# Layer 0's feed-forward of a hybrid S5, retention and attention block: side work at 0.36 and 0.7 steps per yield in place of 0.5 and 0.9

## The chip, the cores and the metric

The kernel runs on one core of a Trainium2 chip, as one program. The metric is the time of the program on the device in microseconds. The kernel before took 1546.05 us, the median of 3 runs (1538.01 to 1549.89).

## The reference, cut to what matters

Two layers work on 256 latent and 256 context tokens of width 1024, all in float32. What bears on the change: each layer's modulation (shift, scale and gate, for both halves of the layer) is a product of two vectors with a 1024 x 6144 matrix; each layer's S5 mixer needs tables that depend on parameters alone; and each layer ends with a SwiGLU feed-forward of hidden width 2816.

```python
for l in range(DEPTH):                       # DEPTH = 2
    mod = (silu_c @ w_ada[l] + b_ada[l])[:, None, :]
    mod_c = silu_cc @ w_ada[l] + b_ada[l]
    sh1, sc1, g1, sh2, sc2, g2 = jnp.split(mod, 6, axis=-1)
    h = rms_norm(x) * (1.0 + sc1) + sh1      # the same for ctx with mod_c
    u, rk, rv, nk, nv, rq, rg, nq, gates = split_cols(h @ w_in[l], IN_SPLIT)
    y_s5, y_s5_c = s5_mixer(u, cu, s5_lam_re[l], ..., need_ctx)
    ...                                      # retention and neighbourhood attention
    x = x + g1 * merge_branches(y_s5, y_ret, y_na, gates, ...)
    x = x + g2 * swiglu(rms_norm(x) * (1.0 + sc2) + sh2, w_ffn_gate[l], w_ffn_up[l], w_ffn_down[l])
return rms_norm(x) * final_norm

def s5_discretize(lam_re, lam_im, log_dt, b_re, b_im): ...   # powers of A and A-scaled B: the tables
def swiglu(h, w_gate, w_up, w_down):
    return (jax.nn.silu(h @ w_gate) * (h @ w_up)) @ w_down
```

In layer 0 the feed-forward is done for both streams (512 tokens), in layer 1 for the latent tokens alone.

## The kernel before, in words

**Products.** Every large product is made of three passes. A weight tile of 128 x 1024 values is loaded by SP's queue (line 377) into one of four raw buffers that are used in turn; ScalarE rounds it into a high part (387), VectorE takes the low part as the difference (388), into one of three pairs of buffers; and TensorE multiplies high by high, high by low and low by high (393 to 395). A product of one weight tile with 512 tokens is 24 matmuls.

**The feed-forward** (`ffn`, 1752) is a generator. For three groups of 8, 8 and 6 hidden tiles it makes the gate and the up projection of each tile, activates and multiplies them (1775 to 1780), and then adds the down projection of the group to the stream (`to_stream`, 1715; residual, 1711). The last down projection of layer 0 leaves its last three output tiles for the end and does them for the context half first, then calls the norm of layer 1 on that half, then does the latent half. It yields after each projection, once for both of the first tile. Behind the feed-forward, layer 1 begins with the norm of the latent half (962), the rest of the last table generator (965), and the first two projections of its keys (971), whose first half of columns needs the context norm alone.

**Side work.** Two chains of steps are woven into layer 0's feed-forward at line 1024. `weave` (204) adds a rate to a counter for each yield of the main generator, and takes one step of the side for each whole unit; what is left when the main generator has ended is done at once:

```python
    for _ in main:
        for i, (_, each) in enumerate(sides):
            acc[i] += each
            while live[i] and acc[i] >= 1.0:
                acc[i] -= 1.0
                step(i)
    while any(live):
        ...
```

The first side, `rest` (1019), makes layer 1's S5 tables. `s5_e` (764) is a state table of a block of groups: one step of six VectorE instructions (756, 757, 759, for two directions), then four steps of four transposes and a copy (776, 778). `s5_kwins` (1181) takes two steps for each of four blocks: a window table of six VectorE instructions (756, 757, 761) from two loaded inputs (683 to 685), then 32 small matmuls (1165), copies, and stores of the window (1178) and of the table (1192). `rest` has the transposes of block 0, blocks 1 and 2 whole, the four windows, and the first step of block 3: 4 + 5 + 5 + 8 + 1 = 23 steps. The transposes of block 3 are what layer 1 does at line 965.

The second side is layer 0's last gate (`ada`, 554; 5 steps) and then `ada_sum` (558) for five of layer 1's six pieces of the modulation. A piece is eight chunks of the matrix. Each chunk is loaded into one of the same four raw buffers, and scaled and added into two accumulators, one for each stream: by ScalarE for the first chunk (568), by VectorE for the others (570, two instructions of 128 x 1024). A ninth step closes the piece with 16 small matmuls (576), a copy, two transposes (540) and the bias (546).

**The order of the instructions.** The order in which the generators run is the order of the program. The framework's planner (`schedule_with_timeline_sim`, 1811) sets each engine's own order from it. Buffers in `fa` are handed out in turn from one arena, so a new buffer waits until what stood in its place has been read.

Of the kernel before, what the change touches and what calls it, by code (L numbers as in the profile page):

```python
# [203 lines left out]
def weave(main, *sides):  # L204

    acc = [0.0] * len(sides)
    live = [True] * len(sides)

    def step(i):
        try:  # L210
            next(sides[i][0])
        except StopIteration:
            live[i] = False
# [8 lines that stand above are left out]
        for i in range(len(sides)):  # L222
            if live[i]:
                step(i)
# [6 lines left out]
def chain(*gens):  # L231
    for g in gens:
        yield from g


class Net:
# [676 lines left out]
    def layer(self, l):  # L913
# [6 lines left out]
        if l == 0:  # L920
# [15 lines left out]
            ada = self.ada(0, (2, 3, 4, 5))  # L936
# [24 lines left out]
        else:  # L961
# [13 lines left out]
            ada = self.adas  # L975
# [18 lines left out]
        ada = self.adas  # L994
        if last:
            ada = self.ada(1, (5,))
            for _ in self.m_out(l):
                pass
            F.cursor = 8192
            self.norm(l, 1, [2, 3])  # L1000
            self.fill(ada, 2, 1)
            weave(self.ffn(l), (ada, 0.5))
        else:
            e = []

            def ahead():
                self.tabs[1] = F.alloc(1280, "p2", top=True), F.alloc(1040, "BB", top=True)
                for blk in range(4):
                    self.et[blk] = F.alloc(2048, "et", top=True)
                b2 = self.s5_tables(1)  # L1010
                yield
                e.extend(self.s5_e(1, b2, blk) for blk in range(4))
                next(e[0])
                yield

            weave(self.m_out(l, lambda: self.norm(l, 1, [0, 1])), (ahead(), 0.5))
            self.norm(l, 1, [2, 3])

            def rest():
                yield from chain(e[0], e[1], e[2], self.s5_kwins(1))  # L1020
                next(e[3])

            self.adas = self.ada_sum(1, range(5))
            weave(self.ffn(l, lambda: self.norm(l + 1, 0, [0, 1])), (rest(), 0.5), (chain(ada, self.adas), 0.9))
            self.e_left = e[3]
        self.dump(f"xffn{l}", self.xT)

# [816 lines left out]
```

## Time and profile before

| | |
|---|---|
| runs shown | 1538.01, 1546.05, 1549.89 us |
| the profiled execution | 1546.39 us, span 1544.6 us |
| TensorE busy | 1492.7 us, 97% of the span |
| VectorE busy | 984.1 us, 64% |
| ScalarE busy | 626.9 us, 41% |
| DMA queue of the weights (q1) | 247.36 MB, 48.4% of 16 engines' span |

The times in the rows are microseconds from the start of the span, on one core. Engines are PE (TensorE matmuls), PEld (its weight loads), DVE (VectorE), ACT (ScalarE), POOL (GpSimd) and SP (the queue that issues loads and stores); a q behind a name is the engine's own queue of waits. Layer 0's feed-forward lies between about 600 and 987 us.

### The profile page before, as it was taken

The page shows a single profiled execution, that of the slowest core. Times are in us where ns is not written, and L with a number is a line of the kernel's source. Part 1 is how long each engine was busy: PE and PEld are TensorE (multiplying, and loading weights), DVE is VectorE, ACT ScalarE, POOL GpSimd, SP SyncE. Part 2 cuts the span into 40 slices and gives each one's busy share as a digit, 9 for nine tenths or more (in the row PEclk, how much of TensorE's full clock was granted, in tenths as well). Part 3 has the DMA queues.
Part 4 walks back from the last instruction along what each step waited for, and adds up shares of the span by engine and source line. Part 5 has one row for each costly group of instructions (what it writes and reads, how often), then busy time and mean ns, then how long its engine had stood idle before and what let it go on. Part 6 is the DMA issues. An engine that isn't in the chain of part 4 may idle for free. (4 is left out here: it accounts for less than half of the span.)

```text
span 1544.6 us, 25494 instructions
## 1 busy us (share of the span) xinstructions
PE 1492.7 (97%) x10066; PEld 1269.3 (82%) x10066; DVE 984.1 (64%) x1729; ACT 626.9 (41%) x1121; POOL 259.5 (17%) x612
## 2 busy tenths in 40 slices
PE   7998898999999999999999999999999999999997
PEld 5886676788888888787887788898689899899997
DVE  6884754445356686598599974732565676665666
ACT  4554443334312334332322322454654355444443
POOL 6206996000000000000000000007991000000000
PEclk9999899999999999999999999999999999999999
DMA  9514456873332533455466642432325667555552
GB/s 369 190 55 141 159 208 176 278 258 113 123 102 69 164 96 111 167 186 178 153 205 214 230 160 65 157 123 75 101 83 161 230 225 271 179 192 184 171 190 98
DMA packets 80760, 255.35 MB, mean 165 GB/s; under 512 B 9216, under 2 KB 23040, under 8 KB 77824
## 3 DMA queue, kind: packets, MB, share of 16 engines
q1 hardware_dynamic: 78016, 247.36, 48.4%
q10 hardware_dynamic: 2304, 4.20, 0.8%
q0 software_dynamic: 320, 2.16, 0.6%
q8 instruction: 79, 1.29, 0.3%
q14 instruction: 41, 0.34, 0.1%
HBM read 230.68 MB, written 20.84 MB: 163 GB/s over the span
## 5 line engine op out<-in xcount | busy, mean ns | idle before, releaser
L393 PE MATMUL psall<-ra 128*128 128x256 f32 (+1 forms) x2122 | 711.3, 340 | 6.1 <-ACT ra L387 2.4
L394 PE MATMUL psall<-ra 128*128 128x256 f32 (+1 forms) x2122 | 709.0, 336 | 0.0
L395 PE MATMUL psall<-ra 128*128 128x256 f32 (+1 forms) x2122 | 707.4, 336 | 1.0 <-DVE ra L388 1.0
L388 DVE TENSOR_TENSOR ra<-fa,ra 128x1024 fp32r<-128x1024 f32 (+1 forms) x284 | 344.8, 1216 | 293.1 <-ACT ra L387 285.9
L387 ACT CAST ra<-fa 128x1024 fp32r<-128x1024 f32 (+1 forms) x284 | 293.7, 1038 | 557.9 <-PE psall L394 336.0
L393 PEld LDWEIGHTS psall<-ra 128*128 128x128 f32 x2122 | 401.7, 191 | 63.2 <-issue 10.7
L395 PEld LDWEIGHTS psall<-ra 128*128 128x128 f32 x2122 | 404.0, 191 | 44.9 <-issue 2.7
L394 PEld LDWEIGHTS psall<-ra 128*128 128x128 f32 x2122 | 405.2, 191 | 39.0 <-issue 1.3
L1109 POOL TENSOR_TENSOR fa<-fa 128x64 f32<-128x64 f32 x252 | 106.1, 442 | 137.4 <-ACT fa L1083 127.7
L1064 POOL MEMSET fa<- 128x32 f32 x2 | 0.2, 123 | 730.2 <-DVE ra L846 730.2
L570 DVE SCALAR_TENSOR_TENSOR fa<-fa 128x1024 f32<-128x1024 f32 x70 | 87.6, 1281 | 9.3 <-DMA fa<-in_wst_dram 7.6
L887 PE MATMUL psall<-ra 128*128 128x512 f32 x192 | 77.8, 414 | 0.2 <-ACT fa L1051 0.2
L888 PE MATMUL psall<-ra 128*128 128x512 f32 x192 | 76.2, 397 | 0.0
L1711 DVE SCALAR_TENSOR_TENSOR fa<-psall,fa 128x256 f32<-128x256 f32 x96 | 43.2, 480 | 51.3 <-PE psall L395 51.1
L889 PE MATMUL psall<-ra 128*128 128x512 f32 x192 | 75.3, 399 | 0.3 <-DVE ra L846 0.3
L1112 POOL TENSOR_TENSOR fa<-fa 128x64 f32<-128x64 f32 x126 | 58.2, 462 | 0.0
L1113 POOL TENSOR_TENSOR fa<-fa 128x64 f32<-128x64 f32 x126 | 53.8, 427 | 9.9
L887 PEld LDWEIGHTS psall<-ra 128*128 128x128 f32 x192 | 43.7, 229 | 8.0 <-issue 2.0
L889 PEld LDWEIGHTS psall<-ra 128*128 128x128 f32 x192 | 43.4, 229 | 6.5 <-DVE ra L846 0.8
L756 DVE TENSOR_TENSOR fa<-fa 128x1024 f32<-128x1024 f32 (+1 forms) x32 | 41.1, 1316 | 11.2 <-PE psall L1165 8.8
L888 PEld LDWEIGHTS psall<-ra 128*128 128x128 f32 x192 | 44.2, 230 | 4.9
L757 DVE TENSOR_TENSOR fa<-fa 128x1024 f32<-128x1024 f32 (+1 forms) x32 | 41.0, 1292 | 2.7 <-DMA fa<-in_s5c_dram 2.7
(242 smaller groups left out, 1380.5 us busy)
## 6 DMA issues: line engine op xcount, KB each, us to landing
fa<-in_wst_dram SPq DMA_DIRECT2D x364, 512.0 KB
gsp<-fa SPq DMA_DIRECT2D x8, 1152.0 KB
fa<-gsp SPq DMA_DIRECT2D x8, 1152.0 KB
fa<-in_wst_dram SPq DMA_DIRECT2D x16, 384.0 KB
xsp<-fa SPq DMA_DIRECT2D x2, 2048.0 KB
tgs<-fa ACTq DMA_DIRECT2D x16, 256.0 KB
fa<-kws SPq DMA_DIRECT2D x32, 128.0 KB
fa<-tgs SPq DMA_DIRECT2D x16, 256.0 KB
```

The costliest lines, as they stand in the source:

```text
L387: nc.scalar.copy(hi[:, :n], t[:, :n])
L388: nc.vector.tensor_tensor(out=lo[:, :n], in0=t[:, :n], in1=hi[:, :n].bitcast(F32), op=ALU.subtract)
L393: mm(out, wh, xh, start=start, stop=False)
L394: mm(out, wh, xl, start=False, stop=False)
L395: mm(out, wl, xh, start=False, stop=stop)
L570: nc.vector.scalar_tensor_tensor(out=acc[s].ap, in0=t, scalar=c, in1=acc[s].ap, op0=ALU.mult, op1=ALU.add)
L887: mm(o, xh, hi[:, ws], start=(kk == 0), stop=False)
L888: mm(o, xh, lo[:, ws], start=False, stop=False)
L889: mm(o, xl, hi[:, ws], start=False, stop=(kk == 7))
L1109: e.tensor_tensor(out=t[:, i], in0=at(pf, pr), in1=tab[:, i * 64:(i + 1) * 64].rearrange("p (r d g) -> p r d g", r=2, d=2), op=ALU.mult)
L1112: e.tensor_tensor(out=at(cf, cr), in0=at(cf, cr), in1=t[:, 0], op=ALU.add)
L1113: e.tensor_tensor(out=at(cf, cr), in0=at(cf, cr), in1=mk(T[s % 2], 96, [[-32, 2], [16, 2], [1, 16]]), op=ALU.add)
```

## The change

Both rates at which the side work is woven into layer 0's feed-forward are lowered: that of the tables from 0.5 to 0.36 steps per yield, and that of the last gate and the weighted sums from 0.9 to 0.7. Nothing else is changed.

```diff
             self.adas = self.ada_sum(1, range(5))
-            weave(self.ffn(l, lambda: self.norm(l + 1, 0, [0, 1])), (rest(), 0.5), (chain(ada, self.adas), 0.9))
+            weave(self.ffn(l, lambda: self.norm(l + 1, 0, [0, 1])), (rest(), 0.36), (chain(ada, self.adas), 0.7))
             self.e_left = e[3]
```

## Rows read from the trace of the kernel before

**Rows 1.** Page: the span, and busy time of each engine over it.

```profile
span 1544.6 us, 25494 instructions
...
PE 1492.7 (97%) x10066; PEld 1269.3 (82%) x10066; DVE 984.1 (64%) x1729; ACT 626.9 (41%) x1121; POOL 259.5 (17%) x612
```

**Rows 2.** Stretches of layer 0's feed-forward and the border behind it, all engines.

```profile
core 0: us, PE busy (x) PEld busy (x) DVE busy (x) ACT busy (x) POOL busy (x), PEclk, DMA share, GB/s
640.00:760.00 120.00, 120.00 (x564) 97.12 (x563) 87.71 (x96) 39.31 (x51) 0.00 (x0) 1.00 0.52 169
760.00:885.00 125.00, 122.39 (x660) 96.72 (x659) 116.03 (x127) 36.59 (x48) 0.00 (x0) 1.00 0.64 214
885.00:952.00 67.00, 67.00 (x309) 54.67 (x308) 39.89 (x48) 18.70 (x25) 0.00 (x0) 1.00 0.40 133
952.00:987.00 35.00, 35.00 (x209) 31.22 (x208) 18.95 (x40) 12.90 (x24) 0.00 (x0) 1.00 0.28 87
987.00:1007.00 20.00, 17.19 (x117) 16.32 (x116) 18.31 (x56) 11.78 (x25) 0.25 (x2) 0.91 0.53 198
```

**Rows 3.** Source lines: duration min/median/max, first and last start, L1711 from 848 on.

```profile
L1711 DVE SCALAR_TENSOR_TENSOR fa<-psall,fa x16: 471/476/484, 854.4 to 887.0; 128x256 f32<-128x256 f32 x16
...
L570 DVE SCALAR_TENSOR_TENSOR fa<-fa x70: 1276/1280/1286, 640.6 to 907.7; 128x1024 f32<-128x1024 f32 x70
...
L756 DVE TENSOR_TENSOR fa<-fa x14: 1214/1351/1358, 617.4 to 881.0; 128x1152 f32<-128x1152 f32 x8, 128x1024 f32<-128x1024 f32 x6
```

**Rows 4.** Stretches, the middle product line L394 alone: TensorE and its weight loads.

```profile
840.00:880.00 40.00, 18.15 (x47) 8.76 (x47) 1.00 0.66 223
880.00:952.00 72.00, 40.46 (x104) 19.33 (x103) 1.00 0.40 135
```

**Rows 5.** Stretches, the weighted sum L570 alone: VectorE, clock, DMA.

```profile
760.00:885.00 125.00, 39.51 (x32) 1.00 0.64 214
885.00:952.00 67.00, 12.48 (x10) 1.00 0.40 133
```

**Rows 6.** Groups of VectorE instructions by shape, 590 to 990 us.

```profile
L570 DVE SCALAR_TENSOR_TENSOR fa<-fa 128x1024 f32<-128x1024 f32 x70 | 87.6, 1281 | 9.3 <-DMA fa<-in_wst_dram 7.6 <-ACT fa L568 1.4
L388 DVE TENSOR_TENSOR ra<-fa,ra 128x1024 fp32r<-128x1024 f32 x61 | 74.5, 1222 | 37.0 <-ACT ra L387 37.0
...
L761 DVE SCALAR_TENSOR_TENSOR fa<-fa 128x1152 f32<-128x1152 f32 x8 | 11.3, 1412 | 0.0
L757 DVE TENSOR_TENSOR fa<-fa 128x1152 f32<-128x1152 f32 x8 | 10.8, 1352 | 0.0
L756 DVE TENSOR_TENSOR fa<-fa 128x1152 f32<-128x1152 f32 x8 | 10.7, 1353 | 1.4 <-PE psall L1165 1.4
...
L757 DVE TENSOR_TENSOR fa<-fa 128x1024 f32<-128x1024 f32 x6 | 7.3, 1219 | 0.0
L759 DVE TENSOR_TENSOR fa<-fa 128x1024 f32<-128x1024 f32 x6 | 7.3, 1219 | 0.0
L756 DVE TENSOR_TENSOR fa<-fa 128x1024 f32<-128x1024 f32 x6 | 7.1, 1218 | 0.4 <-PE psall L776 0.4
```

**Rows 7.** Timeline of TensorE, 846 to 860 us.

```profile
849.81 1.11 PE L1165 MATMUL psall<-fa 128*32 128x128 f32 x30 [0.32 <-DVE fa L761]
...
851.93 1.07 PE L576 MATMUL psall<-fa 128*32 128x256 f32 x16 [1.01 <-DVE fa L1171]
...
858.02 0.50 PE L395 MATMUL psall<-ra 128*128 128x512 f32 x1 [1.03 <-DVE ra L388]
```

**Rows 8.** Waits of SP's queue, 600 to 1010 us: total, times, longest.

```profile
SPq L377 <- DVE fa L570: 69.0, 33, 3.8
...
SPq L1178 <- DVE fa L1174: 8.5, 4, 3.4
```

**Rows 9.** Timeline of ScalarE, 840 to 862 us.

```profile
846.07 0.60 ACT L1775 ACTIVATE fa<-psall 128x512 f32<-128x512 f32 x1 [10.51 <-DVE fa L757]
```

**Rows 10.** Stretch of the border ahead of the feed-forward, columns as in rows 2.

```profile
580.00:600.00 20.00, 17.73 (x141) 14.89 (x139) 15.03 (x48) 9.93 (x19) 0.00 (x0) 0.87 0.43 136
```

## The prediction

> **What bounds the kernel now.** I read the page first, then the feed-forward of layer 0 by stretches of time, then the instructions that the change moves, and last the waits. The span is 1544.6 us and TensorE is busy for 97% of it [rows 1]; the profiled execution took 1546.39 us, 0.3 above the median of the runs shown, so the sum below, made against 1546.4, holds for the median as well. TensorE is the bound, so a new order of the side work can only give back time in which TensorE stood still, or take more.
>
> The reader should look in the stretches for where that is [rows 2]. TensorE is busy without a break from 640 to 760 and from 885 to 987 us. It loses time in two places: between 760 and 885 (122.39 of 125), and at the border to layer 1, 987 to 1007 (17.19 of 20, clock 0.91). VectorE tells why. From 760 to 885 it is busy for 116.03 of 125 us, 93%: there the tables of the four convolution windows and the modulation sums fall together. Behind that, from 885 to 987, it does 39.89 + 18.95 = 58.8 of 102 us, so 43.2 us are free. From 987 to 1007, under the norm that opens layer 1, it is busy for 18.31 of 20: nothing more fits there. So the quiet stretch stands just ahead of a full one, and the change fills the quiet one.
>
> **What is moved, and by how much.** The feed-forward of layer 0 yields 66 times: 15, 16 and 12 for its three groups of hidden columns, and 8, 8 and 7 for the down projections behind them. The table side needs 23 steps. At 0.5 it ends at yield 46, at 0.36 at yield 64 (23 / 0.36 = 63.9). The sums are 50 steps: 5 for layer 0's last gate and 9 for each of five pieces. At 0.9 they end at yield 56. At 0.7 they would need 71.4 yields, so only 46 steps are out at yield 66; the last three chunks of the fifth piece and its closing product come after the feed-forward, **ahead of the norm of line 962**. The sums do not end with it; they run over. Nothing is added or removed: the same instructions, loads and stores are issued in another order.
>
> Yield 47 is the end of the second down projection, whose residuals run to 887.0 [rows 3]. So yields 47 to 66 are the stretch from 885 to 987. A projection is eight triples of matmuls at 0.692 us (104 in 72 us, from 880 to 952 [rows 4]), 5.5 us, one yield. VectorE's work there changes so:
> - Out of it go the 10 weighted sums that stand in it now, 12.5 us [rows 5], and the rest of the fourth state table, 2 x 1.219 [rows 6]: 15 us.
> - Into it come steps 34 to 50 of the sums. The first chunk of a piece is a product on ScalarE, so these are 14 chunks of two instructions: 28 x 1.281 = 35.9 us [rows 6].
> - Three of the four window tables, each 2 x (1.353 + 1.352 + 1.412) = 8.23 us, 24.7 in all, and the whole fourth state table, 2 x (1.218 + 1.219 + 1.219) = 7.3 us [rows 6].
> - In all 67.9 - 15 = 52.9 us more, against 43.2 us free: 9.7 too many, if everything stays in its place.
>
> It does not all stay there. In the trace work starts ahead of its place when VectorE is free: the last weighted sum, due at yield 55 (885 + 8 x 5.5 = 929 us), starts at 907.7, and the first table instruction, due at yield 10 (11 for the first yield of two projections and 9 x 5.5, from 600: about 660), at 617.4 [rows 3]. At 21 us, which is 2.7 steps of the new rate, the sums take 2.36 two-instruction chunks out, 6.1 us; and the first of the three tables, due at yield 48, fits into 760 to 885, which has room: of its 116.0 us go 39.5 of sums [rows 5], 32.9 of window tables and 4.9 of the fourth state table, and 31.4 of sums (14 steps) and 8.2 of one table come, 78.3 in all. That is 9.7 - 6.1 - 8.2 = 4.6 us to spare. But VectorE was busy for 93%, not 100%, where it was fullest. At 93% 102 us hold 94.7, and 7.3 - 4.6 = **2.7 us** spill past 987, where every microsecond of VectorE delays the norm that TensorE waits for. Bounds: 0, and 9.7 + 7.3 = 17.0 if nothing moves ahead. I take 2.7, since these rows show work moving ahead.
>
> **What is given back.** Between 760 and 885 the free time of TensorE is 2.6 us. By spacing it is more: from 840 to 880 there are 47 triples [rows 4], 47 x 0.692 = 32.5 us, and with two blocks of 30 small matmuls at 1.11 and 16 at 1.07 [rows 7] 35.8 us are accounted for, 4.2 lost. The waits there name VectorE: the split of a weight (L388) 1.03 and the end of a window (L1171) 1.01 [rows 7]. I take 2.6 of 4.2 (bounds 0 and 4.2), because the fuller late stretch can bring part of the same waits back.
>
> **The rest.** The weight splits of layer 1's first two projections, 2 x 1.222 [rows 6], come behind the norm in the order of the program: 0 while they find gaps in its chain, 2.4 if not; I take 0, as the chain's gaps hold them now. TensorE's own side products move and stay as many; they cost the same. Also moved later are the four stores of windows and four of tables, and the loads of table inputs, on SP. A window's store holds weight loads queued behind it, 8.5 us in four, longest 3.4, and the sums hold them 69.0 us in 33 [rows 8]; three weight buffers, two projections of work ahead, cover that now, and 3.4 is the price where the cover is gone. POOL has no part (nothing in these stretches before 987 [rows 2]). The two accumulators of the sums stay allocated to the end, so other buffers come round sooner; such a reuse made ScalarE wait 10.51 us for a table instruction once [rows 9]. This is priced with the spill.
>
> The border already runs at 0.91 of the clock for 20 us after 2.8 us of idle time, 1.8 us lost (3.6 us at 1.2 GHz in place of 2.4); the border ahead of the feed-forward shows 0.87 after 2.3, 2.6 lost [rows 10]. Between 760 and 885 the clock stays at 1.00 in spite of the 2.6 idle. I add 0 for the clock: more idle time did not go with a lower clock in these two. Bounds 0 and 2.6. The Trainium skill, "TensorE: Matmul & The Clock Gate", section "HAM oscillation — how this bites in real kernels", speaks against the change: idle stretches between bursts of matmuls bring the clock down to half, and it is paid again on the way up. By that rule, idle time gathered at the border costs once more what it costs there now, an estimate of 1.8 us, and the sum would be 1548.3 and not 1546.5.
>
> **Sum:** 1546.4 - 2.6 + 2.7 = 1546.5; I say **1547**.
>
> **Rivals.**
> 1. *Spill at the border* (slower). VectorE keeps the sums' tail and the fourth state table in front of the norm; nothing moves ahead because buffers are not free. 17.0 + 2.4 + 2.6 - 2.6 = 19.4, so 1565.8 at the worst; with half of the spill, 8.5 + 2.4 + 1.8 - 2.6, 1556.5. It decides once VectorE has more than about 95 us of work between 885 and 987. For it: 18.31 of 20 behind, and the tail that runs over. Against: work starts 21 to 43 us early now.
> 2. *All waits go* (faster). Nothing spills, 4.2 come back in the middle and 1 of the 2.8 at the border: 1541.2. For it: from 640 to 987 VectorE has 262.6 of 347 us of work with either order, 76% [rows 2]. Against: the border's waits are a chain, not a load. "Perfetto Trace Analysis", section "Optimization Strategy", of the Trainium skill says that interleaving stretches with different limits may help; the trace shows only these 4.2 us to be had by it.
> 3. *It does not do what it says*: since the order of instructions follows when they can start, the new rates change little of what runs when: 1546, plus or minus 2.
>
> **Numbers.** Forecast (cancelling) 0.50, rival 1 0.27, rival 2 0.13, rival 3 0.10. About 1% (15.5 us) is what a measurement can tell from no change. More than that faster would need more idle time than 760 to 1007 holds (2.6 or 4.2, and 2.8, and 1.8 of clock): 0.03. Slower by over 1% is the upper part of rival 1, and stalls that a new order brings later in layer 1: 0.16. Within: 0.81. The range goes from rival 2 less half the spread of the runs shown, 1537, to 1563, most of rival 1.
>
> **What would show it.** Right: VectorE near 75 to 90 of 125 us from 760 to 885 and above 90 of 102 from 885 to 987; window tables and weighted sums still after 930; no idle TensorE in the middle; 3 to 6 us idle at the border. Wrong: weighted sums among the norm's instructions with more than 10 us of idle TensorE behind them, or tables still early with the same waits in the middle.

## The result, and the profile after

The kernel after takes 1555.18 us, the median of 20 runs (1546.37 to 1557.95); the kernel before, in 20 runs beside it, 1541.95 (1533.94 to 1549.89). The ratio is 1.0073, with a 95% interval from 1.0058 to 1.0087: 0.7% slower, about 11 us (the two medians alone lie 13.2 us apart). That lies inside 1% and inside the range, but it is not nothing. The profiled execution of after took 1550.7 us, 4.5 below its median, and that of before 4.4 above its own, so the two traces differ by only 4.3 us. In the trace of after layer 0's feed-forward starts 4.9 us earlier (608.4 against 613.3), in a part that the change does not touch; from there on after is 9.1 us longer.

The page of after: the span and each engine's busy time, as [rows 1].

```profile
span 1548.8 us, 25486 instructions
...
PE 1492.8 (96%) x10066; PEld 1271.6 (82%) x10066; DVE 988.9 (64%) x1729; ACT 627.3 (41%) x1121; POOL 259.6 (17%) x612
```

TensorE did the same work in the same busy time; the new microseconds are idle. The stretches of after show where, with the columns of [rows 2]:

```profile
760.00:885.00 125.00, 125.00 (x603) 100.63 (x602) 90.99 (x102) 36.16 (x46) 0.00 (x0) 1.00 0.51 174
885.00:952.00 67.00, 67.00 (x361) 53.84 (x360) 50.98 (x60) 21.98 (x31) 0.00 (x0) 1.00 0.51 162
952.00:987.00 35.00, 28.03 (x206) 23.75 (x206) 34.44 (x47) 10.38 (x20) 0.00 (x0) 0.87 0.75 267
987.00:1007.00 20.00, 14.87 (x83) 13.53 (x84) 15.84 (x56) 9.59 (x22) 0.25 (x2) 0.72 0.08 30
```

Between 760 and 885 us TensorE no longer stands still (125.00 of 125, against 122.39), and VectorE came down from 116.03 to 90.99. From 952 to 1007 TensorE is idle for 12.1 of 55 us, at 0.87 and 0.72 of the clock; before it was 2.8, at 1.00 and 0.91. By source line, with the columns of [rows 3], first the residual from 848 us on and then the weighted sum:

```profile
L1711 DVE SCALAR_TENSOR_TENSOR fa<-psall,fa x24: 462/472/484, 850.7 to 975.3; 128x256 f32<-128x256 f32 x24
...
L570 DVE SCALAR_TENSOR_TENSOR fa<-fa x70: 1265/1279/1286, 642.8 to 980.6; 128x1024 f32<-128x1024 f32 x70
```

The last residual of the feed-forward starts at 975.3 and the last weighted sum behind it, at 980.6. In before the sums ended at 907.7 [rows 3], and the last residual started at 988.3 (the row in [rows 3] covers the residuals of the first two groups alone). That residual in the timeline of VectorE in before (start, duration, line):

```profile
988.28 0.48 DVE L1711 SCALAR_TENSOR_TENSOR fa<-psall,fa 128x256 f32<-128x256 f32 x1
```

The gain in the middle is seen in the product line alone, as [rows 4]:

```profile
840.00:880.00 40.00, 21.03 (x54) 10.15 (x54) 1.00 0.62 212
```

54 triples in place of 47 between 840 and 880 us, 7 x 0.692 = 4.8 us of product. Not all of that is idle time won: in before 64 small matmuls of line 1165 took 3.03 us in this stretch, in after 22 of them take 1.16. The weighted sums by stretch, as [rows 5]:

```profile
760.00:885.00 125.00, 29.98 (x24) 1.00 0.51 174
885.00:952.00 67.00, 12.48 (x10) 1.00 0.51 162
952.00:987.00 35.00, 12.39 (x10) 0.87 0.75 267
```

24 sums in place of 32 in the full stretch, the same 10 in the next, and 10 from 952 on, where before had none. The border on TensorE, first in the timeline of before (start, duration, line, in brackets the idle time and its releaser), from the feed-forward's last product:

```profile
987.56 0.28 PE L395 MATMUL psall<-ra 128*128 128x256 f32 x1
987.68 1.47 PE L776 MATMUL psall<-fa 128*128 128x128 f32 x12
988.99 0.28 PE L801 MATMUL psall<-fa 128*128 128x1 f32 x2
990.20 0.83 PE L801 MATMUL psall<-fa 128*128 128x1 f32 x6 [0.92 <-ACT fa L794]
991.78 0.70 PE L827 MATMUL psall<-fa 128*128 128x256 f32 x2 [0.76 <-ACT fa L822]
993.59 0.51 PE L393 MATMUL psall<-ra 128*128 128x256 f32 x2 [1.11 <-ACT ra L845]
```

and in that of after:

```profile
973.72 0.28 PE L395 MATMUL psall<-ra 128*128 128x256 f32 x1
979.23 1.08 PE L576 MATMUL psall<-fa 128*32 128x256 f32 x8 [5.23 <-DVE fa L570]
981.90 1.08 PE L576 MATMUL psall<-fa 128*32 128x256 f32 x8 [1.59 <-DVE fa L570]
983.04 2.82 PE L776 MATMUL psall<-fa 128*128 128x128 f32 x12
985.96 0.69 PE L540 MATMUL psall<-fa 128*128 128x128 f32 x2
986.44 1.78 PE L801 MATMUL psall<-fa 128*128 128x1 f32 x8
991.12 1.22 PE L827 MATMUL psall<-fa 128*128 128x256 f32 x2 [2.90 <-ACT fa L822]
993.45 0.80 PE L393 MATMUL psall<-ra 128*128 128x256 f32 x2 [1.11 <-ACT ra L845]
```

Before, 6.03 us lie between the last product of layer 0 (987.56) and the first of layer 1 (993.59); after, 19.73 (973.72 to 993.45): 13.7 more. Their parts can be read off. **Waits** were 0.92 + 0.76 + 1.11 = 2.79 and are 5.23 + 1.59 + 2.90 + 1.11 = 10.83: 8.0 more, of which 6.82 are the closing product of the fifth piece (line 576) waiting for its weighted sums. **Work that lay inside the feed-forward before**: that product and its two transposes. Inside the feed-forward the 16 matmuls of such a product take 1.07 us (after, at 937.25) and two transposes of line 540 take 0.38 (before, at 706.39), 1.45 together. **The clock**: here the same matmuls take 2 x 1.08 and 0.69, 1.4 more; twelve transposes take 2.82 in place of 1.47, the small sums of line 801 1.78 in place of 0.28 + 0.83, line 827 1.22 in place of 0.70, these three together 2.5 more. So the clock makes 3.9, and the three parts 13.4 of 13.7. The timeline of VectorE in after, over the same time, shows what the waits are for:

```profile
974.86 0.86 DVE L1711 SCALAR_TENSOR_TENSOR fa<-psall,fa 128x256 f32<-128x256 f32 x2
...
976.78 1.21 DVE L757 TENSOR_TENSOR fa<-fa 128x1024 f32<-128x1024 f32 x1
977.91 1.27 DVE L570 SCALAR_TENSOR_TENSOR fa<-fa 128x1024 f32<-128x1024 f32 x1
...
980.58 1.27 DVE L570 SCALAR_TENSOR_TENSOR fa<-fa 128x1024 f32<-128x1024 f32 x1
981.77 1.21 DVE L759 TENSOR_TENSOR fa<-fa 128x1024 f32<-128x1024 f32 x1
...
984.05 2.25 DVE L796 TENSOR_TENSOR fa<-fa 128x256 f32<-128x256 f32 x5
```

From 975.64, where the residuals are done, to 984.05 VectorE is busy without a gap with state tables (757, 759), sums (570) and weight splits (388), before it gets to the squares of the norm (796), but for one of them at 980.24.

For the runs that follow, four lengths were read from each trace. **ffn** is from ScalarE's wait ahead of the first activation of layer 0's feed-forward (line 1775; the activation itself starts 0.8 to 0.9 us later) to the start of its last residual (line 1711). **Norm** is from there to the start of the last normed tile of layer 1 (line 846). **Late** is the duration of the weighted sums and table instructions that start on VectorE in the last 20 us ahead of that residual, plus those behind it. The last column goes from that same wait to the first copy of layer 1's first projection (line 1041).

| kernel | ratio to before [95%] | ffn | late | norm | activation to projection |
|---|---|---|---|---|---|
| before | 1 | 375.8 | 0 | 17.6 | 416.6 |
| after | 1.0073 [1.0058, 1.0087] | 367.7 | 15.0 + 4.9 | 34.7 | 423.9 |
| e1, tables at the new rate only | 0.9969 [0.9947, 0.9992] | 368.7 | 4.9 | 18.1 | 412.0 |
| e2, sums at 0.7, tables at 0.48 | 1.0004 [0.9980, 1.0027] | 371.1 | 10.2 | 24.0 | 416.6 |
| e3, sums at 0.78 | 0.9990 [0.9970, 1.0010] | 369.2 | 3.7 | 21.2 | 411.9 |
| e4, leftover steps behind the norm | 1.0090 [1.0063, 1.0117] | 368.8 | 13.9 + 5.0 | 37.1 | 427.8 |
| e5, closing product behind the norm | 1.0085 [1.0059, 1.0112] | 367.8 | 15.2 + 5.0 | 38.8 | 428.4 |
| e6, last state table by layer 1 | 1.0026 [1.0002, 1.0050] | 369.3 | 11.5 + 7.3 | 28.6 | 419.7 |
| e7, half sums | 0.9998 [0.9975, 1.0022] | 365.4 | 11.2 + 1.3 | 28.3 | 415.4 |
| e8, half sums at 0.9 | 0.9944 [0.9920, 0.9968] | 368.0 | 4.9 | 18.9 | 410.6 |
| e9, before, fifth piece held back | 1.0032 [1.0012, 1.0053] | 377.7 | 7.7 | 24.3 | 423.5 |
| e10, half sums at 0.9, tables at 0.42 | 0.9955 [0.9932, 0.9979] | 367.6 | 0 | 17.9 | 409.0 |
| e11, half sums at the rates of before | 0.9982 [0.9960, 1.0004] | 372.5 | 0 | 17.6 | 414.0 |
| e12, half sums, accumulators in turn | 0.9979 [0.9956, 1.0001] | 365.2 | 11.2 | 25.3 | 412.1 |

After against before: 8.1 us won in the feed-forward, 17.1 lost in the norm, 1.7 won between the norm and the projection, 7.3 in all. The rest of layer 1, up to TensorE's last matmul, took 1.8 more in the trace (509.0 against 507.2), which is less than that length varies between the traces (505.2 to 511.8). So 7.3 of the measured 11 are accounted for, and the remaining 4 can't be told from that variation. What the last column differs by from before agrees in each of the thirteen kernels with what its ratio makes of 1542 us, to about 4 us (after 7.3 and 11, e3 -4.7 and -1.5, e8 -6.0 and -8.6).

### The profile page after: what moved, and what is told of

It reads as the page before. It is cut to its first block, busy times and chain, and to the rows that moved or that the text cites. A ratio compares the mean times of both kernels' runs of the same rounds, so it can differ in the third digit from the quotient of the medians.

```text
span 1548.8 us, 25486 instructions
## 1 busy us (share of the span) xinstructions
PE 1492.8 (96%) x10066; PEld 1271.6 (82%) x10066; DVE 988.9 (64%) x1729; ACT 627.3 (41%) x1121; POOL 259.6 (17%) x612
## 4 chain that ended last, share of the span: by engine, by line
PE 77%; DVE 3%; DMA 1%; ACT 1%; issue 0%; DVEq 0%; ACTq 0%
PE psall L393 21%; PE psall L395 21%; PE psall L394 21%; PE psall L887 2%; PE psall L889 2%; PE psall L888 2%; PE psall L1227 1%; PE psall L1587 1%; PE psall L1601 1%; PE psall L1380 1%; PE psall L526 1%; PE psall L1075 1%; PE psall L1415 1%; DMA fa<-kws 1%; DVE fa L570 1%; PE psall L1387 1%
## 5 line engine op out<-in xcount | busy, mean ns | idle before, releaser
L394 PE MATMUL psall<-ra 128*128 128x256 f32 (+1 forms) x2122 | 709.3, 336 | 0.0
L394 PEld LDWEIGHTS psall<-ra 128*128 128x128 f32 x2122 | 405.5, 191 | 39.2 <-issue 0.9
L570 DVE SCALAR_TENSOR_TENSOR fa<-fa 128x1024 f32<-128x1024 f32 x70 | 87.3, 1279 | 17.2 <-DMA fa<-in_wst_dram 16.0
L1711 DVE SCALAR_TENSOR_TENSOR fa<-psall,fa 128x256 f32<-128x256 f32 x96 | 43.1, 478 | 51.4 <-PE psall L395 51.3
```

Source lines behind the costliest of these rows:

```text
L394: mm(out, wh, xl, start=False, stop=False)
L570: nc.vector.scalar_tensor_tensor(out=acc[s].ap, in0=t, scalar=c, in1=acc[s].ap, op0=ALU.mult, op1=ALU.add)
```

## The experiments

The expectations number some theories. Theory 1 is that VectorE's total between 885 and 990 us decides. Theory 4, formed after the first runs, is that only what VectorE still has to do of the side work in the last 20 us decides. Theory 6 is that the single pair of accumulators keeps the fifth piece from starting early. The others are named by what they say.

**Each half alone.** e1 keeps the tables at 0.36 and puts the sums back to 0.9; e2 keeps the sums at 0.7 and puts the tables at 0.48.

```diff
-            weave(..., (rest(), 0.36), (chain(ada, self.adas), 0.7))
+            weave(..., (rest(), 0.36), (chain(ada, self.adas), 0.9))      # e1
+            weave(..., (rest(), 0.48), (chain(ada, self.adas), 0.7))      # e2
```

> Tables at 0.36 as after the change, sums at 0.9 as before, so the sums end at yield 56 and nothing of them is left at the border. Theory 1 (VectorE's backlog at the border: more work between 885 and 987 us than fits): only the tables, about 29 us, come into 43 us of free time, so no spill: ratio to before 0.995 to 1.000. Rival 1 (the closing product of the sums, queued on TensorE ahead of the norm, is what stops it): it is gone here too, 0.995 to 1.000. Rival 2 (the cost is in the later tables, or in other stages, not in the sums): 1.005 to 1.008.

> Sums at 0.7 as after the change, tables at 0.48, so that they end at yield 48 (46 before; 0.5 itself finds no room for its buffers beside the slower sums). Four steps of the sums still run over the feed-forward's end, and the closing product still stands ahead of the norm. Theory 1 (VectorE's backlog): 23 us more come into 43 us of free time, little or no spill: 0.997 to 1.002. Rival 1 (place of the closing product): still slow, 1.004 to 1.008. Rival 2 (later tables): 0.997 to 1.000.

Measured: e1 0.9969 [0.9947, 0.9992], a little faster than before; e2 1.0004 [0.9980, 1.0027], no change. Neither half costs what the two cost together. The stretches of e1:

```profile
760.00:885.00 125.00, 124.95 (x609) 101.69 (x608) 99.49 (x110) 37.29 (x47) 0.00 (x0) 1.00 0.60 196
...
952.00:987.00 35.00, 32.71 (x222) 28.11 (x222) 29.93 (x76) 16.75 (x34) 0.00 (x0) 0.91 0.51 184
987.00:1007.00 20.00, 19.34 (x127) 18.67 (x126) 12.12 (x25) 10.97 (x20) 0.25 (x2) 0.99 0.27 72
```

It has the whole gain in the middle (124.95 of 125; ffn 7.1 shorter) and nearly none of the loss: with its sums out by 898.9 us, 4.9 us of tables are late, and the norm ends 18.1 us after the last residual. In e2 the sums still run to 981.4, but the tables are out of the way, so 10.2 us are late and the norm ends at 24.0. Together the two sides leave twice as much late work as the sums alone.

**The order of the program at the border.** The closing product of line 576 stands ahead of the norm's products on TensorE, so its place could be the cost, rather than VectorE's load. e4 does the leftover steps (three chunks and the closing product) only behind layer 1's first norm and weight loads; e5 does the closing product alone there.

```diff
-            weave(self.ffn(...), (rest(), 0.36), (chain(ada, self.adas), 0.7))
+            self.late = chain(ada, self.adas)
+            weave(self.ffn(...), (rest(), 0.36), (self.late, 0.7), drain=False)   # e4
...
             kpre = self.pair([("ws", l, O_NK + m * 128) for m in range(2)])
+            for _ in self.late:            # e4
+                pass
+            self.ada_close(1, 4)           # e5, with the closing product taken out of ada_sum for piece 4
```

> As after the change, but what is left of the sums at yield 66 (three chunks and the closing product) is issued in layer 1 behind the first two key projections, so behind the norm. Theory 1 (VectorE's backlog): 7.7 us less of VectorE's work ahead of the norm, the fourth state table stays: 1.000 to 1.004. Rival 1 (place of the closing product): the whole loss goes, 0.995 to 1.000. Rival 2 (later tables): 1.005 to 1.008.

> As after the change, but the closing product of the fifth piece alone (16 small matmuls, a copy, two transposes and the bias) is issued behind the first two key projections; all of VectorE's weighted sums stay ahead of the norm. Theory 1 (VectorE's backlog): TensorE waits for the norm's sums in place of the closing product, 1.005 to 1.008 as after the change. Rival 1 (place of the closing product): the loss goes, 0.996 to 1.001. Rival 2 (later tables): 1.005 to 1.008.

Measured: 1.0090 [1.0063, 1.0117] and 1.0085 [1.0059, 1.0112], as slow as after. TensorE's waits from 978 us on in e5 (line numbers 12 higher there: 788 is 776, 771 is 759):

```profile
990.27 1.75 PE L788 MATMUL psall<-fa 128*128 128x128 f32 x7 [9.07 <-DVE fa L771]
993.58 1.87 PE L813 MATMUL psall<-fa 128*128 128x1 f32 x8 [1.55 <-DVE fa L808]
```

The closing product has left the path, and TensorE waits 9.07 us for a state table instead. So the place of line 576 on TensorE is not the cause: whatever comes first behind VectorE's queue takes the wait. e4 did not put its edit to the test: moving steps in the program did not move them on VectorE. The planner still ran two of the three late chunks at 975 to 983 us; only the last came behind, its second sum at 997.3 us. TensorE's timeline in e4 has a wait of the same kind and about the same size as in e5:

```profile
990.08 1.75 PE L776 MATMUL psall<-fa 128*128 128x128 f32 x7 [7.92 <-DVE fa L759]
```

**Amount or lateness.** e3 lets the sums end at yield 65, within the feed-forward. e6 takes the last state table (block 3) out of the side work, so that layer 1 makes it whole, behind the border. e7 and e8 leave out the context stream's sums of the last three pieces, which layer 1, where the context is not updated, does not use; e7 at the rates of after, e8 at 0.36 and 0.9.

```diff
-            weave(..., (rest(), 0.36), (chain(ada, self.adas), 0.7))
+            weave(..., (rest(), 0.36), (chain(ada, self.adas), 0.78))     # e3
+            weave(..., (rest(), 0.36), (chain(ada, self.adas), 0.9))      # e8, with e7's edit
...
-                next(e[3])                                                # e6
...
-                for s in range(2):
+                for s in range(1 if r > 1 else 0, 2):                     # e7, e8
```

> Tables at 0.36, sums at 0.78, so that the last step of the sums falls on yield 65 of 66: nothing runs over, but the sums stay dense to the end. Theory 1 (VectorE's backlog at the border): between the tables with sums at 0.9 (0.997) and the change (1.007), nearer to the change, as only about two chunks are done earlier: 1.003 to 1.007. Rival 3 (the overrun behind yield 66 alone costs): 0.995 to 0.999.

> As after the change, but the first step of the fourth state table (six VectorE instructions, 7.3 us) is left to layer 1, behind the norm, where its transposes already are. Theory 1 (VectorE's backlog): 7.3 us less ahead of the norm, 1.000 to 1.004. Rival 3 (the overrun of the sums): 1.006 to 1.009, as the sums are not touched.

> Rates as after the change; the weighted sums for the context stream are left out for the last three of the five pieces (layer 1 reads these for the latent stream alone), 21 instructions of 1.28 us, 14 of them among steps 34 to 50; loads, order and closing products stay (the closing products of these pieces have 8 matmuls, not 16). Theory 1 (VectorE's backlog): 17.9 us less of VectorE's work between yield 47 and the norm, more than the spill: 0.993 to 0.999. Rival 3 (the overrun, or the place of the tail): 1.004 to 1.008, since all of it stays where it is.

> The half sums of the run before with tables at 0.36 and sums at 0.9. Theory 1: a little under the tables alone (0.997), since what VectorE still delays ahead of the border is smaller: 0.992 to 0.997. Rival 3: as the tables alone, 0.996 to 0.998.

Measured: e3 0.9990 [0.9970, 1.0010], e6 1.0026 [1.0002, 1.0050], e7 0.9998 [0.9975, 1.0022], e8 0.9944 [0.9920, 0.9968]. The stretches of e3 decide against theory 1:

```profile
885.00:952.00 67.00, 67.00 (x361) 54.09 (x360) 54.80 (x61) 20.51 (x29) 0.00 (x0) 1.00 0.52 170
952.00:987.00 35.00, 31.94 (x234) 27.23 (x233) 30.41 (x66) 16.36 (x33) 0.00 (x0) 0.97 0.54 196
```

The line of its weighted sums:

```profile
L570 DVE SCALAR_TENSOR_TENSOR fa<-fa x70: 1273/1280/1287, 641.6 to 941.8; 128x1024 f32<-128x1024 f32 x70
```

VectorE has 54.80 + 30.41 = 85.2 us of work from 885 to 987, as after has (50.98 + 34.44 = 85.4), but the sums end at 941.8, 3.7 us are late and the norm ends at 21.2 in place of 34.7. Counted back from each kernel's own last residual it is the same: VectorE is busy for 83.7 of the last 100 us in e3 and for 82.7 in after. The same amount of work costs 13.5 us less when it is done in time. e6 moves 7.3 us of tables behind the border and e7 takes 7.4 us of late work away; each gives back 6 us of the norm. e8, with half sums that also end early, has the lowest ratio of all, though its interval overlaps those of e1 and e10.

**Lateness alone, and the gain alone.** e9 is the kernel before with one edit: the fifth piece waits until the 60th yield, with all else early as before. e11 is the kernel before with e7's edit, so that VectorE is thinner in the middle and nothing is late. e10 is e8 with the tables at 0.42.

```diff
-            weave(self.ffn(...), (rest(), 0.5), (chain(ada, self.adas), 0.9))
+            weave(counted(self.ffn(...), count), (rest(), 0.5),
+                  (held(chain(ada, self.adas), 41, count, 60), 0.9))      # e9
...
+            weave(..., (rest(), 0.42), (chain(ada, self.adas), 0.9))      # e10, with e7's edit
-                for s in range(2):
+                for s in range(1 if r > 1 else 0, 2):                     # e11, on before
```

> The kernel before with both of its rates, but the fifth piece of the sums (9 steps, 7 chunks of two weighted sums) is held back until yield 60 of 66. Theory 4 (what counts is the side work that VectorE still has in the last 20 us of the feed-forward and behind it; the norm's end moves by about as much): some 10 to 15 us of it stand there, so the norm ends 8 to 13 us later than before, nothing is gained in the middle: 1.004 to 1.009. Theory 1 as first put (the total between 885 us and the border): the total is the same as before, 0.999 to 1.001.

> Half sums (none for the context stream in the last three pieces), sums at 0.9, tables at 0.42, so the tables end at yield 55. Theory 4: no side work is left in the last 20 us (4.9 us with 0.36), the norm's end comes at most 1 us earlier, so as with 0.36: 0.992 to 0.996. If the state table's transposes at the border cost by themselves: 0.990 to 0.993.

> The kernel before with both of its rates and the half sums alone (21 weighted sums of 1.28 us fewer). Theory 5 (what the change gains ahead of the border, 8 us, is VectorE's full stretch between 760 and 885 us being thinned out): VectorE falls there from 116 to about 98 us, and the feed-forward gets 5 to 8 us shorter with nothing lost at the border: 0.994 to 0.997. Rival 5 (the gain comes of something else that the rates move, not of VectorE's load): 0.999 to 1.001.

Measured: e9 1.0032 [1.0012, 1.0053], e10 0.9955 [0.9932, 0.9979], e11 0.9982 [0.9960, 1.0004]. The stretches of e9:

```profile
885.00:952.00 67.00, 67.00 (x298) 55.44 (x297) 31.57 (x38) 20.82 (x26) 0.00 (x0) 1.00 0.34 105
952.00:987.00 35.00, 34.33 (x215) 29.93 (x214) 27.10 (x38) 9.96 (x17) 0.00 (x0) 1.00 0.53 164
```

VectorE is less than half busy from 885 to 952 (31.57 of 67) and has less to do from 885 to 987 than after (58.7 against 85.4), and yet the norm ends 6.7 us later than in before: 7.7 us of late sums, 1.0032, a little under what was expected. That is the dose for one late piece without any other change. The fullest stretch of e11 gives the other side:

```profile
760.00:885.00 125.00, 124.92 (x657) 98.99 (x656) 101.78 (x120) 35.09 (x48) 0.00 (x0) 1.00 0.65 216
```

VectorE falls from 116.03 to 101.78 us between 760 and 885, TensorE is busy for 124.92, and the ffn is 3.3 us shorter: in the right direction, less than was expected. A thinner VectorE in the middle gives back a part. With the tables at 0.36 the gain is 7.1 (e1), though VectorE is hardly thinner there than in e11 (99.49 against 101.78); by what way the lower rate gives the rest is not shown. e10, with nothing late and a thin middle, shows both together: ffn 367.6, norm 17.9.

**Why nothing moved ahead.** VectorE had 16 of 67 us free between 885 and 952 in after. The timeline of VectorE in after has the fourth piece's last sums and the fifth's first:

```profile
911.51 2.48 DVE L570 SCALAR_TENSOR_TENSOR fa<-fa 128x1024 f32<-128x1024 f32 x2
...
939.14 1.29 DVE L570 SCALAR_TENSOR_TENSOR fa<-fa 128x1024 f32<-128x1024 f32 x1 [0.90 <-ACT fa L568]
```

TensorE's timeline has the closing product of the fourth piece:

```profile
937.25 1.07 PE L576 MATMUL psall<-fa 128*32 128x256 f32 x16
```

And ScalarE's the first product of the fifth:

```profile
937.96 1.15 ACT L568 ACTIVATE fa<-fa 128x1024 f32<-128x1024 f32 x1 [1.30 <-PE psall L576]
```

The fourth piece's last sum is done at 914.0. Its closing product stands on TensorE at 937.25, where the program put it. The fifth piece's first product writes the same accumulators, and so ScalarE waits for it (1.30 us to 937.96) and the first sum of the fifth piece runs at 939.14. For 25 us VectorE had no sum that it could do. e12 gives the last pieces an accumulator in turn (with e7's half sums, so that the two there are suffice):

```diff
-            b = acc[s]                         # e7: acc[s], written out in each use
+            b = acc[r % 2 if r > 1 else s]     # e12
```

> Half sums at the rates of the change (0.36 and 0.7), and the last three pieces take the two accumulators in turn, so that the fifth piece need not wait until TensorE has closed the fourth at its place in the program (it did so 943 to 944 us into the span in the run with half sums, 28 us after the fourth piece's last sum). The instructions and their number stay. Theory 6 (that closing product is what holds the fifth piece back and so puts it into the last 20 us): the fifth piece starts 10 to 25 us earlier, less than 8 us of side work is left in the last 20 us (12.5 with half sums), the norm ends 4 to 8 us earlier: 0.994 to 0.998. Rival 6 (the sums are held by their loads, which share four raw buffers with the weights): the fifth piece starts at most 5 us earlier, 0.999 to 1.001.

Measured: 0.9979 [0.9956, 1.0001], against 0.9998 [0.9975, 1.0022] of e7. The sums of e12 (line 571 there) on VectorE:

```profile
908.56 1.28 DVE L571 SCALAR_TENSOR_TENSOR fa<-fa 128x1024 f32<-128x1024 f32 x1 [3.73 <-DMA fa<-in_wst_dram]
...
929.01 2.61 DVE L571 SCALAR_TENSOR_TENSOR fa<-fa 128x1024 f32<-128x1024 f32 x2 [1.58 <-DMA fa<-in_wst_dram]
...
954.53 1.28 DVE L571 SCALAR_TENSOR_TENSOR fa<-fa 128x1024 f32<-128x1024 f32 x1
...
970.02 1.27 DVE L571 SCALAR_TENSOR_TENSOR fa<-fa 128x1024 f32<-128x1024 f32 x1
```

and of e7:

```profile
914.88 1.28 DVE L570 SCALAR_TENSOR_TENSOR fa<-fa 128x1024 f32<-128x1024 f32 x1 [3.35 <-DMA fa<-in_wst_dram]
...
944.54 1.28 DVE L570 SCALAR_TENSOR_TENSOR fa<-fa 128x1024 f32<-128x1024 f32 x1 [0.90 <-ACT fa L568]
...
980.30 1.28 DVE L570 SCALAR_TENSOR_TENSOR fa<-fa 128x1024 f32<-128x1024 f32 x1
```

The feed-forward of e12 starts 6.7 us earlier in its span than that of e7 (first activation at 608.7 and 615.4), so the two are compared from there. So counted, the fifth piece's first product, on ScalarE, comes 23.3 us earlier (913.4 against 943.4 in the spans), its first sum on VectorE 8.8 earlier (929.0 against 944.5), and VectorE is through the sums 3.6 earlier (971.3 against 981.6). So the accumulators did hold the piece back. But little of that reaches its end: the wait named ahead of the first sums is now that for their load (1.58 <-DMA), five of the sums still run from 954.5 on, 11.2 us stay late, and the norm ends at 25.3, 3.0 earlier; the intervals of the two ratios overlap. Theory 6 is shown for the start of the piece and not for the whole effect; that the loads hold the sums, the rival put against it, is refuted for the start and open for the rest.

## Why the prediction was right or wrong

The time fell inside the range, within 1% and on its slower side, but that is luck more than insight: the range reached to most of rival 1, and the sum itself did not hold. It put the change at +0.1 us where about 11 were measured, and it came as near as that only because two of its terms were wrong in opposite directions: 8.1 given back in place of 2.6 made up for a part of 17.1 spilt in place of 2.7. The case that was held likeliest, cancelling at 0.50, is not what happened; rival 1, at 0.27, is nearer.

- **What bounds the kernel.** Right: TensorE's busy time did not change (1492.7 and 1492.8 us), and all that happened is idle time and clock.
- **What is given back, 2.6.** Mis-sized: 8.1 was measured (ffn 375.8 to 367.7). Where an instruction of TensorE started over 0.15 us later than is the median behind one of its kind, the excess was added up: 11.7 us in the feed-forward of before, 5.8 in that of after, without the border's first wait. So 5.9 are gaps that are gone: 4.2 at 840 to 860 (4.6 to 0.4), as [rows 4, 7] had bounded them, and the rest in small gaps that no wait names. The other 2 have the size of TensorE's side work that now stands behind the feed-forward (16 small matmuls of line 576 and 8 of line 801, about 1.1 us each): moved, not won. "The fuller late stretch can bring part of the same waits back" did not come true.
- **The spill, 2.7.** This step failed, and it failed at "since these rows show work moving ahead", which was read as if all of the work could. Some did move ahead: of the 28 weighted sums put between 885 and 987, 20 ran there (12.48 + 12.39 us), and VectorE was busy for 85.4 of 102 us, not for the 94.7 that were taken. By the sum's own measure nothing should have spilt. But it took the 102 us as one store, in which free time anywhere counts. The rows showed 21 us of advance *inside* a piece; between pieces the closing product holds the accumulators, and in after it held the fifth piece for 25 us, so that 16 us stayed free early and a backlog stood at the end. Measured: 17.1 us, the upper bound of 17.0 "if nothing moves ahead". That the two agree so closely is partly chance, since the bound held no term for the closing product and the clock, which the 17.1 contain. (The 2.36 chunks that the sum took ahead are 2.1 if 7 of a piece's 9 steps are such chunks, 5.4 us in place of 6.1; its spill is then 3.4 and not 2.7, which changes nothing here.)
- **The clock, 0.** Wrong: 3.9 us in the gap alone, above the bound of 2.6. The clock was at its lower level, 1.2 GHz in place of 2.4, for some 20 us: 0.87 from 952 to 987 is about 9 us of it, 0.72 from 987 to 1007 about 11, so from about 978 to 998. In before it was 3.6 us (0.91 of 20 [rows 2]). The stretch from 984 to 994 lies wholly inside. After:

```profile
984.00:994.00 10.00, 5.89 (x23) 4.53 (x21) 6.90 (x27) 4.79 (x11) 0.00 (x0) 0.50 0.45 181
```

And before, in the same stretch:

```profile
984.00:994.00 10.00, 7.21 (x56) 6.53 (x55) 9.18 (x33) 6.10 (x12) 0.00 (x0) 1.00 0.64 229
```

Before the clock fell TensorE had stood still since its last product, which ended at 974.0; up to 983.0 it did 16 small matmuls and nothing else. The row of [rows 10] on which the 0 was rested had 2.3 us of idle time, not 10.8. What the Trainium skill says in "TensorE: Matmul & The Clock Gate", section "HAM oscillation — how this bites in real kernels", holds here: idle time brings the clock down and is paid for again on the way up. The 1.8 us estimated by it were nearer than the 0 that was taken.
- **The rest.** The weight splits "0 while they find gaps in its chain" stand at 975.64, 979.11 and 982.91 in the backlog, 1.21 each; they were not tested by themselves. SP's queue is as predicted: loads held by the sums 68.2 us in 32, against 69.0 in 33 [rows 8].
- **The signs.** "No idle TensorE in the middle" came true, VectorE from 760 to 885 was 90.99, just over the 75 to 90. Weighted sums stood after 930 too (939.14 to 980.58). "Above 90 of 102" and "3 to 6 us idle at the border" did not (85.4, 12.1). "Weighted sums among the norm's instructions with more than 10 us of idle TensorE behind them" was the sign given for a wrong forecast, and it is what the trace shows (10.83 us of waits).
- **The rivals.** What happened is rival 1, the spill at the border, at its full size, and with its reason ("nothing moves ahead because buffers are not free") for the fifth piece, together with rival 2's first half, all waits gone in the middle. Neither excludes the other, and the sum treated them as if they did. Rival 1's full price with the larger gain is 17.0 + 2.4 + 2.6 - 8.1 = 13.9, against 11 measured. Its point of decision, "more than about 95 us of work between 885 and 987", was wrong: e3 has the same 85 us without the loss, and e9 has a loss at 58.7. Rival 3, no effect, is refuted by the stretches.
- **The dose.** Over the table the norm's end grows with the late work: 4.9 us cost 0.5 to 1.3, 7.7 cost 6.7, 10.2 to 12.5 cost 6.4 to 10.7, and 18.9 to 20.2 cost 17.1 to 21.2 (e6 lies below this with 11.0 for 18.8, of which 7.3 are behind the border, and e3 above with 3.6 for 3.7). Where 5 us are late, the border's gaps can hold most of it; at 20 nearly every microsecond is paid.

Left open: what in layer 1 makes its length vary between 505 and 512 us from trace to trace; how much of the late work an earlier fifth piece would save at full sums, since a second pair of accumulators was not tried; what holds that piece's sums once its accumulators are free; and what the small pieces of the gain are.

## What to carry to other kernels

Side work that is spread over a stage must be out some way ahead of the stage's end: an engine that is free on the average (85 of 102 us) can still have 20 us of backlog at the border, and the next stage waits for nearly all of it. Before "it will start early" is put into a sum, look for what a piece must wait for, here the accumulators that the piece ahead of it gives back only at its closing product. Of the two rates only one was worth changing: e1, the tables alone at 0.36, is 0.3% faster than before, and with the unused sums left out e8 and e10 are 0.5% faster.

## What the runs showed of the hardware

A backlog on VectorE is paid twice: the 10.8 us of waits in the 20 us of the border brought TensorE's clock to its lower level for some 20 us (0.87 of the stretch from 952 to 987, 0.72 of that from 987 to 1007), and there two matmuls of line 827 took 1.22 us in place of 0.70; 3.9 of the 13.7 us are of this kind. In before, e1 and e10, where TensorE waits at the border for about 3 us (0.92 + 0.76 + 1.11, 1.7 + 0.7 + 0.3 and 1.4 + 1.1 + 0.8), the same stretches make it about 3.6, 6.7 and 6.9 us at the lower level: shorter, but not none. Those of e10:

```profile
952.00:987.00 35.00, 31.72 (x203) 28.82 (x202) 24.45 (x67) 15.76 (x33) 0.12 (x1) 0.93 0.50 172
987.00:1007.00 20.00, 20.00 (x125) 19.78 (x125) 14.00 (x29) 12.19 (x22) 0.13 (x1) 0.95 0.29 93
```
